# S5's parameters on GpSimd, and partition changes by TensorE products

## The chip, the core and the metric

The kernel runs on one core of one Trainium2 chip. The metric is the device time of one execution in microseconds (us). The core has a matrix engine (TensorE, PE in the profile; PEld is its weight load), three engines for elementwise work (VectorE or DVE, ScalarE or ACT, GpSimd or POOL) and a queue engine for transfers (SyncE or SP). Each of them takes its instructions in the order in which they stand in its queue, and waits at semaphores for the others. SBUF is the on-chip memory of 128 partitions, PSUM holds what TensorE produces.

## The reference

A decoder of two layers over 272 tokens (16 learned ones and 256 of the input), width 1024, in float32. In every layer the normed input is projected by one large matrix `w_in`; four mixers work on slices of the result, each is gated and projected back, and a squared-ReLU MLP follows.

```python
def s5_mixer(u, lam_re, lam_im, b_re, b_im, c_re, c_im, d_skip, log_step, glu_w, glu_b):
    step = exp(log_step)[:, None]
    mag = exp(lr * step)
    ab_re, ab_im = mag * cos(li * step), mag * sin(li * step)
    inv = 1.0 / (lr * lr + li * li)
    co_re = ((ab_re - 1.0) * lr + ab_im * li) * inv
    co_im = (ab_im * lr - (ab_re - 1.0) * li) * inv
    # bb = co * b (complex); x_t = ab * x_{t-1} + bb u_t; y_t = Re(c x_t)
    y = y.reshape(bsz, t, BRANCH_WIDTH) + d_skip * u
    y = gelu(y)
    a, gt = split(y @ glu_w + glu_b, 2, axis=-1)
    return a * sigmoid(gt)

def rotary(x):      # retention's q and k, heads of 64
    x1, x2 = x[..., :half], x[..., half:]
    return concatenate([x1 * cos - x2 * sin, x1 * sin + x2 * cos], axis=-1)
```

S5's parameters (`ab`, `co`, and powers of `ab`) depend on the weights alone: 32 groups of 64 states, for both layers. The other two mixers are a Mamba-2 SSD and HGRN2.

## The kernel before, in words

Activations are kept with features on the partitions and the 272 tokens along the free axis. Weights arrive in 336 chunks of 128 x 1024 floats (`wst`), in a fixed order (`ORDER`): in each layer HGRN's inputs, SSD's, S5's, HGRN's gate, then gates and branch products of the mixers, retention's inputs, the GLU, the output product and the MLP. Each chunk is split into a high part on ACT (`whi`, L325) and a low part on DVE (`wlo`, L327), with three and two buffers. Every product with a weight chunk is then three matmuls, high by high, high by low and low by high (L344, L345, L347). So for each chunk PE needs one ACT and one DVE operation, and these stand in their engines' queues among all the other work.

The program is written in the order hgrn_in, hgrn, ssd_in, ssd, s5_params (layer 0 only, for both layers), s5_in, s5, gates and merges, ret_in, ret, glu. The order of the instructions in each queue isn't that order: a planner (`schedule_with_timeline_sim`) sets it from its own estimate of times, with offsets of priority (`PS`, `PD` for chunks), and it mixes chunks with the mixers' small steps. Once set, each queue's order is fixed.

`s5_params` (L833) computes the parameters on [128, 2, 16] slices: sine and cosine by polynomials, powers of `ab` in `pw`, coefficients `c5`, and tables `eb`, `ea` that are doubled in length step by step. Its helpers `tt` and `ts` are a two-input operation (L845) and one with scalars (L849, L851). HGRN's level updates (L1324) and SSD's decay products (L1442) are on POOL.

`s5` (L1090) runs four batches of four pairs of groups. `s5_prep` loads raw weights (`s5a`, DMA issued on ACT's queue), makes `bs`, `cx` and the tables `s5e` (`s5_table`, on POOL); `s5_run` multiplies by the input (L1109, into two PSUM banks of tag "mb"), runs the recurrence as two scans on DVE and adds up the output Y (L1148). Within Y a partition holds (position in a block of 4 tokens, feature), so after every second batch `s5_out` (L1150) applies Gelu on ACT and copies 16 pieces of 32 partitions to other partitions of `yf`, eight on ACT (L1162) and eight on DVE (L1160). At the end `split` (L362 on ACT, L364 on DVE) makes the high and low parts that the GLU reads much later.

`ret_in` (L1476) copies q and k out of PSUM, loads two tables of cosines and sines, and on POOL makes four products of 32 partitions each that write to the neighbouring 32 partitions (L1496), one product over all (L1497) and two adds (L1500 for q, L1501 for k into `kpad`).

Of the kernel before, what the change touches and what calls it, by code (L numbers as in the profile page):

```python
# [12 lines left out]
AF = mybir.ActivationFunctionType  # L13
ALU = mybir.AluOpType
# [54 lines left out]

CONSTS = {}  # L70
_n = 0
for _name, _w in (("ident", 128), ("ones", 128), ("cen", 128), ("m432", 432), ("he", 1), ("ho", 1), ("le", 1), ("lo", 1),
                  ("rh", 1), ("rl", 1), ("r1", 1)):
    CONSTS[_name] = (_n, _w)
    _n += _w
# [18 lines left out]
def shape_constants():  # L94
    f = np.float32
    p = np.arange(128)
    c = np.zeros((128, NCONST), f)

    def put(name, a):
        o, w = CONSTS[name]  # L100
        c[:, o:o + w] = a

    put("ident", np.eye(128))
    put("ones", 1.0)
    put("cen", np.eye(128) - 1.0 / 128)
    t = np.arange(T)
    m = np.zeros((128, 432))
    m[:, :272] = t[None, :] >= p[:, None]
    m[:, 272:416] = t[None, 128:] >= 128 + p[:, None]
    m[:, 416:] = (t[None, 256:] >= 256 + p[:, None]) & (p[:, None] < 16)  # L110
    put("m432", m)
    h, r = p // 16, p % 16

    for nm, odd in (("e", 0), ("o", 1)):
        low = np.where((r == 6) & (h % 2 == odd), -1.0, 0.0)
        put("l" + nm, low[:, None])
        put("h" + nm, (np.where((r == 0) & (h % 2 == odd), -1.0, 0.0) - low)[:, None])
    put("rl", (r >= 6)[:, None])
    put("rh", np.where(r < 6, 1.0, -1.0)[:, None])
    put("r1", ((r == 0) | (r == 6))[:, None])  # L120
    sc = np.zeros((128, NSSDC), f)
    s = np.arange(384)
    chunk, used = r % 6 - 1, (r % 6 > 0) & (r < 12)
    blk = used[:, None] & ((s[None, :] // CH) == chunk[:, None]) & (s[None, :] < T)
    sc[:, 0:384] = blk & (h[:, None] % 2 == 0)
    sc[:, 384:768] = blk & (h[:, None] % 2 == 1)
    sc[:, 768:1040] = used[:, None] & (t[None, :] >= CH * chunk[:, None])
    sc[:, 1040:1312] = (t[None, :] % CH) != 0

    gam = 1.0 - np.exp2(-5.0 - np.arange(4.0))  # L130
    inv = (10000.0 ** (-np.arange(32.0) / 32)).astype(f)
    ang = (t[:, None].astype(f) * inv[None, :]).astype(f).astype(np.float64)
    rot = np.zeros((128, 2, 4, T))
    for i in range(2):
        for q in range(4):
            head = 2 * i + q // 2
            rows = slice(32 * q, 32 * q + 32)
            up = gam[head] ** t.astype(np.float64)
            for k in range(2):
                g = (1.0 / up) * 64 ** -0.5 if k else up  # L140
                rot[rows, 0, 2 * k + i] = np.cos(ang).T * g

                sgn = 1.0 if q % 2 == 0 else -1.0
                rot[rows, 1, 2 * k + i] = sgn * np.sin(ang).T * g
    lv = np.zeros((128, len(LEVELS), 128), np.int32)
    x = p[:, None] ^ p[None, :]
    for i, hh in enumerate(LEVELS):
        if hh == 0:
            lv[:, i] = x == 0
        else:  # L150
            lv[:, i] = (x >= hh) & (x < 2 * hh) & (p[None, :] > p[:, None])
    return c, sc, rot.astype(f).reshape(128, 2 * 4 * T), lv.reshape(128, -1)
# [81 lines left out]
class Net:  # L234
# [598 lines left out]
    def s5_params(self):  # L833

        nc = self.nc
        v = nc.vector
        DD = [128, DEPTH, 16]
        S, S2 = self.s5t("s5b").rearrange("p (i l q) -> p i l q", l=DEPTH, q=16), self.s5t("s5c")
        d4 = S2[:, 256:512]
# [2 lines left out]
        lr, li, step = col("lr"), col("li"), self.stp[:, :, 0:16]  # L842

        def tt(o, a, b, op):
            v.tensor_tensor(out=o, in0=a, in1=b, op=op)  # L845

        def ts(o, a, s1, op0, s2=None, op1=None):
            if op1 is None:
                v.tensor_scalar(out=o, in0=a, scalar1=s1, scalar2=None, op0=op0)  # L849
            else:  # L850
                v.tensor_scalar(out=o, in0=a, scalar1=s1, scalar2=s2, op0=op0, op1=op1)  # L851

        it = iter([S[:, i] for i in range(34)] + [S2[:, i] for i in range(8)])
        new = lambda: next(it)
# [5 lines left out]
        k, r, z, sn, cs = new(), new(), new(), new(), new()  # L860
        ts(k, th, 0.6366197723675814, ALU.mult, MAGIC, ALU.add)
        ts(k, k, MAGIC, ALU.subtract)
        v.scalar_tensor_tensor(out=r, in0=k, scalar=-PIO2[0], in1=th, op0=ALU.mult, op1=ALU.add)
        v.scalar_tensor_tensor(out=r, in0=k, scalar=-PIO2[1], in1=r, op0=ALU.mult, op1=ALU.add)
        v.scalar_tensor_tensor(out=r, in0=k, scalar=-PIO2[2], in1=r, op0=ALU.mult, op1=ALU.add)
        tt(z, r, r, ALU.mult)
        ts(sn, z, SIN_C[0], ALU.mult, SIN_C[1], ALU.add)
        tt(sn, sn, z, ALU.mult)
# [6 lines left out]
        ts(cs, cs, COS_C[2], ALU.add)  # L875
        tt(cs, cs, z, ALU.mult)
        tt(cs, cs, z, ALU.mult)
        v.scalar_tensor_tensor(out=cs, in0=z, scalar=-0.5, in1=cs, op0=ALU.mult, op1=ALU.add)
        ts(cs, cs, 1.0, ALU.add)

        q, odd, ss, sc, d = new(), new(), new(), new(), new()
        ts(q, k, 0.25, ALU.mult, MAGIC, ALU.add)
        ts(q, q, MAGIC, ALU.subtract)
        v.scalar_tensor_tensor(out=q, in0=q, scalar=-4.0, in1=k, op0=ALU.mult, op1=ALU.add)
        tt(d, q, q, ALU.mult)
        ts(odd, d, 1.0, ALU.is_equal)
        ts(d, d, 4.0, ALU.is_equal)
# [17 lines left out]
        tt(cs, Bv, sc, ALU.mult)  # L905

        pw = self.cp.tile([128, 2, 5, DEPTH, 16], F32, name="s5p")
        v.memset(pw[:, 0, 0], 1.0)
        v.memset(pw[:, 1, 0], 0.0)
        tt(pw[:, 0, 1], mag, cs, ALU.mult)  # L910
        tt(pw[:, 1, 1], mag, sn, ALU.mult)

# [7 lines left out]

        P = lambda i: (pw[:, 0, i], pw[:, 1, i])
        cmul(*P(2), *P(1), *P(1))
        cmul(*P(3), *P(2), *P(1))
        cmul(*P(4), *P(2), *P(2))

        c5 = self.cp.tile([128, 2, 4, DEPTH, 16], F32, name="s5c")
        inv, t = new(), new()
# [12 lines left out]
        tt(t, am, li, ALU.mult)  # L940
        tt(cI, cI, t, ALU.subtract)
        tt(cI, cI, inv, ALU.mult)
        for s in (2, 1, 0):
            cmul(c5[:, 0, s], c5[:, 1, s], cR, cI, *P(3 - s))

        self.eb = self.cp.tile([128, 2, DEPTH, 16, 8], F32, name="s5eb")
        self.ea = self.cp.tile([128, 2, DEPTH, 16, 9], F32, name="s5ea")
# [2 lines left out]
        cmul(*e1, *e2, *e2)  # L950
        cur = e1
        for t, n in ((self.eb, 8), (self.ea, 9)):
            v.memset(t[:, 0, :, :, 0:1], 1.0)
            v.memset(t[:, 1, :, :, 0:1], 0.0)
            w = 1
            while w < n:
                k = min(w, n - w)
                sh = [128, DEPTH, 16, k]
                f = [c.unsqueeze(3).to_broadcast(sh) for c in cur]
                src, dst = ([t[:, r, :, :, o:o + k] for r in range(2)] for o in (0, w))  # L960
                tm = d4[:, 0:32 * k].rearrange("p (l q k) -> p l q k", l=DEPTH, q=16)
                tt(dst[0], src[0], f[0], ALU.mult)
                tt(tm, src[1], f[1], ALU.mult)
                tt(dst[0], dst[0], tm, ALU.subtract)
                tt(dst[1], src[0], f[1], ALU.mult)
                tt(tm, src[1], f[0], ALU.mult)
                tt(dst[1], dst[1], tm, ALU.add)
                if t is self.eb or 2 * w < n:
                    nxt = e8 if cur is not e8 else e2
                    cmul(*nxt, *cur, *cur)  # L970
                    cur = nxt
                w *= 2
# [105 lines left out]
        return W.rearrange("p a q c -> p (a q) c")  # L1078

    def s5(self, l, W):  # L1080
        yf = self.slot(6, [128, 4, 68, 4])
        for b in range(4):
            Y = self.cmy[:, 2:4].rearrange("p a (q c) -> p (a q) c", q=4)
            if l and b == 0:
                prep = self.ahead
            else:
                fs, prep = self.s5_prep(l, b, self.decay if l and b == 1 else self.begin)
                for f in fs:
                    f()
            self.s5_run(l, b, W, prep, Y[:, 4 * (b % 2):4 * (b % 2) + 4])  # L1090
            if b % 2:
                self.s5_out(b - 1, Y, yf)
        yf = yf.rearrange("p a c s -> p a (c s)")
        gh, gl = self.slot(9, [128, 4, T], F32R), self.slot(7, [128, 4, T], F32R)
        for i in range(4):
            self.split(yf[:, i], gh[:, i], gl[:, i])
        return gh, gl

    def s5_run(self, l, b, W, prep, Y):
# [47 lines left out]
                                 rhs=st[:, r, q, 0:68], start=False, stop=(r == 1))  # L1147
        v.tensor_tensor(out=Y, in0=yp, in1=du, op=ALU.add)  # L1148

    def s5_out(self, b, Y, yf):  # L1150

        nc = self.nc
        Y = Y.rearrange("p q c -> p (q c)")
        nc.scalar.activation(Y, Y, AF.Gelu_apprx_tanh)
        G = Y.rearrange("p (a q c) -> p a q c", a=2, q=4)
        for q in range(4):
            for s in range(4):
                o, i = yf[32 * q:32 * q + 32, b:b + 2, :, s], G[32 * s:32 * s + 32, :, q, :]
                if q % 2:
                    nc.vector.tensor_copy(o, i)  # L1160
                else:
                    nc.scalar.activation(o, i, AF.Copy)  # L1162

    def glu(self, l, x, ks, sl):
        nc = self.nc
# [313 lines left out]
    def ret_in(self, l, u, t0):  # L1479
# [11 lines left out]
        for i in range(2):  # L1491
            self.load_after(rot[i], self.io["rot"].rearrange("p (c k t) -> p c k t", c=2, k=4)[:, i], qk[:, 0:1, 0:1])
        sw = self.slot(13, [128, 4, T])
        for q in range(4):
            a, b = slice(32 * q, 32 * q + 32), slice(32 * (q ^ 1), 32 * (q ^ 1) + 32)
            g.tensor_tensor(out=sw[b], in0=qk[a], in1=rot[1][a], op=ALU.mult)  # L1496
        g.tensor_tensor(out=qk, in0=qk, in1=rot[0], op=ALU.mult)  # L1497
        qf, k = self.slot(14, [128, 4, T]), self.kpad[1]
        q = qf[:, 0:2]
        g.tensor_tensor(out=q, in0=qk[:, 0:2], in1=sw[:, 0:2], op=ALU.add)  # L1500
        g.tensor_tensor(out=k[:, :, 0:T], in0=qk[:, 2:4], in1=sw[:, 2:4], op=ALU.add)  # L1501
        v01, v2 = self.slot(0, [128, 2, 4, 128]), self.vpad[0].rearrange("p (i e) -> p i e", i=4)
        for i in range(4):
            ps = self.proj(l, O_RV + 128 * i, u)
# [47 lines left out]
```

## Time and profile before

| | |
|---|---|
| median of 3 runs | 1277.0 us (1274.56 to 1277.59) |
| profiled execution | 1277.68 us |
| its span | 1275.9 us |
| PE busy | 1216.1 us, 95% |
| DVE busy | 893.0 us, 70% |
| ACT busy | 694.2 us, 54% |
| POOL busy | 411.0 us, 32% |

The profile is of one execution. Busy time counts an engine's own instructions, without its waits. Matmuls overlap in the pipeline, so the mean of one (about 0.29 us) is longer than the distance to the next (about 0.125 us). A matmul in float32 appears as two records in the trace, each with its weight load; the three products with weight chunks are single records. The chain of waits follows the execution back from its last instruction, at each step to what released it.

### The profile page before, as it was taken

What the parts mean: (1) busy time and instruction counts of PE and PEld (TensorE: products, weight loads), DVE (VectorE), ACT (ScalarE), POOL (GpSimd) and SP (SyncE); (2) the same over time, 40 slices, a digit from 0 to 9 for tenths busy, and PEclk for the clock granted to TensorE, in tenths of its full rate; (3) what the DMA queues carried; (4) which work ended last, traced back from release to release, by engine and by line L of the source; (5) the groups of instructions that cost most, each with busy time, mean ns of one, the idle gap of its engine ahead of it and who ended that gap; (6) DMA issues with size and microseconds to landing.
All of it is one profiled execution on the core that took longest, in us unless ns stands there. A gap on an engine that the chain in (4) does not pass through costs nothing.

```text
span 1275.9 us, 24312 instructions
## 1 busy us (share of the span) xinstructions
PE 1216.1 (95%) x9534; PEld 1174.6 (92%) x9534; DVE 893.0 (70%) x1480; ACT 694.2 (54%) x1219; POOL 411.0 (32%) x422
## 2 busy tenths in 40 slices
PE   8999998879999989999989999988999998999997
PEld 7999897879999989999979998987999998999996
DVE  8999989885637675544468995898656487655444
ACT  7446746443745665544455558354647546665442
POOL 2452467668002142200024333575170031322001
PEclk9999999989999989999989999998999998999998
DMA  6423232344354535555434332333444553555552
GB/s 238 160 98 104 101 123 99 108 136 145 135 175 173 176 110 178 173 175 178 170 108 143 126 123 97 123 111 114 146 150 149 184 179 136 169 188 189 182 184 98
DMA packets 53187, 186.69 MB, mean 146 GB/s; under 512 B 6096, under 2 KB 7248, under 8 KB 53072
## 3 DMA queue, kind: packets, MB, share of 16 engines
q1 hardware_dynamic: 50480, 179.40, 41.2%
q10 hardware_dynamic: 2592, 5.74, 1.4%
q8 instruction: 75, 1.23, 0.4%
q14 instruction: 40, 0.33, 0.1%
HBM read 184.06 MB, written 1.05 MB: 145 GB/s over the span
## 4 chain that ended last, share of the span: by engine, by line
PE 76%; DVE 13%; issue 4%; POOL 3%; ACT 2%; DMA 1%; SPq 0%; DVEq 0%; ACTq 0%; POOLq 0%
PE g L347 22%; PE g L344 22%; PE g L345 22%; DVE wlo L327 3%; PE mb L726 1%; PE ma L1263 1%; PE mb L717 1%; POOL S L1496 1%; DVE h L604 1%; DMA s5a<-in_bc 1%; DVE big_npom L601 1%; DVE s5a L1012 1%; ACT whi L325 1%; PE ma L726 1%; PE mb L1109 1%
## 5 line engine op out<-in xcount | busy, mean ns | idle before, releaser
L327 DVE TENSOR_TENSOR wlo<-wst,whi 128x1024 fp32r<-128x1024 f32 x336 | 438.5, 1306 | 259.1 <-PE g L347 220.8
L325 ACT ACTIVATE whi<-wst 128x1024 fp32r<-128x1024 f32 x336 | 355.8, 1060 | 365.3 <-PE g L345 287.6
L347 PE MATMUL g<-xh_u,wlo 128*128 128x272 f32 (+1 forms) x1024 | 299.7, 294 | 16.0 <-DVE wlo L327 15.8
L344 PE MATMUL g<-xh_u,whi 128*128 128x272 f32 (+1 forms) x1024 | 299.5, 293 | 0.6 <-ACT early L1068 0.4
L345 PE MATMUL g<-xl_u,whi 128*128 128x272 f32 (+1 forms) x1024 | 297.8, 291 | 0.0
L344 PE MATMUL g<-S,whi 128*128 128x272 f32 (+1 forms) x832 | 236.0, 288 | 4.6 <-ACT S L541 4.1
L347 PE MATMUL g<-S,wlo 128*128 128x272 f32 (+1 forms) x808 | 230.0, 288 | 1.7 <-DVE wlo L327 1.7
L345 PE MATMUL g<-S,whi 128*128 128x272 f32 (+1 forms) x768 | 220.4, 289 | 2.2 <-DVE S L552 1.9
L347 PEld LDWEIGHTS g<-xh_u,wlo 128*128 128x128 f32 x1024 | 195.7, 192 | 21.0 <-DVE wlo L327 18.2
L344 PEld LDWEIGHTS g<-xh_u,whi 128*128 128x128 f32 x1024 | 196.5, 192 | 2.6 <-ACT early L1068 0.7
L345 PEld LDWEIGHTS g<-xl_u,whi 128*128 128x128 f32 x1024 | 196.5, 192 | 1.5 <-issue 1.2
L344 PEld LDWEIGHTS g<-S,whi 128*128 128x128 f32 x832 | 157.1, 190 | 5.3 <-ACT S L541 4.5
L347 PEld LDWEIGHTS g<-S,wlo 128*128 128x128 f32 x808 | 151.9, 189 | 2.6 <-DVE wlo L327 2.2
L345 PEld LDWEIGHTS g<-S,whi 128*128 128x128 f32 x768 | 145.8, 190 | 4.1 <-DVE S L552 4.0
L345 PE MATMUL g<-xl_npm,whi 128*128 128x272 f32 (+1 forms) x512 | 147.7, 291 | 1.2 <-DVE xl_npm L552 1.2
L344 PE MATMUL g<-xh_npm,whi 128*128 128x272 f32 (+1 forms) x512 | 143.6, 289 | 2.4 <-ACT xh_npm L541 2.4
L347 PE MATMUL g<-xh_npm,wlo 128*128 128x272 f32 (+1 forms) x496 | 140.5, 288 | 0.0
L345 PEld LDWEIGHTS g<-xl_npm,whi 128*128 128x128 f32 x512 | 99.1, 193 | 1.9 <-DVE xl_npm L552 1.7
L344 PEld LDWEIGHTS g<-xh_npm,whi 128*128 128x128 f32 x512 | 96.7, 193 | 2.9 <-ACT xh_npm L541 2.9
L677 POOL TENSOR_TENSOR acc<-acc,tmp 128x272 f32<-128x272 f32 (+1 forms) x48 | 38.9, 828 | 186.0 <-DVE tmp L676 186.0
L347 PEld LDWEIGHTS g<-xh_npm,wlo 128*128 128x128 f32 x496 | 94.2, 192 | 0.2
L507 POOL TENSOR_TENSOR tmp<-tmp 128x272 f32<-128x272 f32 (+1 forms) x64 | 45.7, 714 | 137.3 <-DVE wlo L327 79.5
(377 smaller groups left out, 2184.4 us busy)
## 6 DMA issues: line engine op xcount, KB each, us to landing
wst<-in_w SPq DMA_DIRECT2D x336, 512.0 KB, 3.5
S<-in_rot ACTq DMA_DIRECT2D x4, 544.0 KB, 6.8
s5a<-in_bc ACTq DMA_DIRECT2D x8, 256.0 KB, 3.4
h<-in_h SPq DMA_DIRECT2D x4, 272.0 KB, 5.5
S<-in_ssdc ACTq DMA_DIRECT2D x2, 384.0 KB, 4.4
dtc<-in_ssdc ACTq DMA_DIRECT2D x2, 272.0 KB, 4.7
out<-h SPq DMA_DIRECT2D x2, 256.0 KB, 2.8
S<-in_lvl SPq DMA_DIRECT2D x1, 448.0 KB, 7.2
```

Source lines behind the costliest of these rows:

```text
L325: a = nc.scalar.activation(hi, st, AF.Copy)
L327: nc.vector.tensor_tensor(out=lo, in0=st, in1=hi.bitcast(F32), op=ALU.subtract)
L344: self.nc.tensor.matmul(out, lhsT=a, rhs=r, start=st, stop=False)
L345: self.nc.tensor.matmul(out, lhsT=a, rhs=s, start=False, stop=False)
L347: end = self.nc.tensor.matmul(out, lhsT=b, rhs=r, start=False, stop=en)
L507: nc.gpsimd.tensor_tensor(out=q, in0=a, in1=a, op=ALU.mult)
L601: e.tensor_tensor(out=mw[:, k], in0=mw[:, k], in1=r, op=ALU.mult)
L604: e.tensor_tensor(out=self.h[:, k, sl], in0=self.h[:, k, sl], in1=mw[:, k], op=ALU.add)
L677: nc.gpsimd.tensor_tensor(out=a, in0=a, in1=t, op=ALU.add)
L717: nc.tensor.matmul(ps[:, c0:c0 + T - q0], lhsT=k[b, 128 * s:128 * s + 128], rhs=q[b, q0:T], start=True, stop=True)
L726: nc.tensor.matmul(out[:, t:T], lhsT=v01[s] if s < 2 else v2, rhs=P[:, p0:p0 + T - t], start=s == 0, stop=s == 2)
L1012: e.tensor_tensor(out=tmp, in0=X[1 - r], in1=F[1], op=ALU.mult)
```

## The change

S5's parameters: the helpers now issue on GpSimd; `scalar_tensor_tensor` becomes two operations each, the third and fourth powers are made in one complex product, and the three `c5` products in one. The reciprocal and the exponential for `mag` stay on VectorE. S5's outputs: `s5_out` no longer copies; for each half of Y it makes 16 matmuls with 32 columns of the identity as weights, which bring the four pieces of 32 partitions to their place in a PSUM bank. After the second batch two ACT copies bring the banks to `yf`; after the fourth the banks are split directly. Retention's rotary: a constant matrix "swap" exchanges the halves by one matmul per tile, DVE multiplies by the sine table (whose sign is now that of the receiving half), POOL multiplies by the cosine table and adds, tile by tile.

```diff
@@ constants
+    put("swap", np.eye(128)[p ^ 32])
...
-                sgn = 1.0 if q % 2 == 0 else -1.0
+                sgn = -1.0 if q % 2 == 0 else 1.0
@@ s5_params
         def tt(o, a, b, op):
-            v.tensor_tensor(out=o, in0=a, in1=b, op=op)
+            g.tensor_tensor(out=o, in0=a, in1=b, op=op)
 
         def ts(o, a, s1, op0, s2=None, op1=None):
...
-                v.tensor_scalar(out=o, in0=a, scalar1=s1, scalar2=s2, op0=op0, op1=op1)
+                g.tensor_scalar(out=o, in0=a, scalar1=s1, scalar2=s2, op0=op0, op1=op1)
...
-        v.scalar_tensor_tensor(out=r, in0=k, scalar=-PIO2[0], in1=th, op0=ALU.mult, op1=ALU.add)
-        v.scalar_tensor_tensor(out=r, in0=k, scalar=-PIO2[1], in1=r, op0=ALU.mult, op1=ALU.add)
-        v.scalar_tensor_tensor(out=r, in0=k, scalar=-PIO2[2], in1=r, op0=ALU.mult, op1=ALU.add)
+        for i, c in enumerate(PIO2):
+            ts(z, k, -c, ALU.mult)
+            tt(r, z, r if i else th, ALU.add)
...
-        cmul(*P(3), *P(2), *P(1))
-        cmul(*P(4), *P(2), *P(2))
+        sh = [128, 2, DEPTH, 16]
+        d = d4[:, 0:64].rearrange("p (i l q) -> p i l q", i=2, l=DEPTH)
+        cmul(pw[:, 0, 3:5], pw[:, 1, 3:5], pw[:, 0, 1:3], pw[:, 1, 1:3],
+             *[x.unsqueeze(1).to_broadcast(sh) for x in P(2)])
...
-        for s in (2, 1, 0):
-            cmul(c5[:, 0, s], c5[:, 1, s], cR, cI, *P(3 - s))
+        sh = [128, 3, DEPTH, 16]
+        d = d4[:, 0:96].rearrange("p (i l q) -> p i l q", i=3, l=DEPTH)
+        cmul(c5[:, 0, 0:3], c5[:, 1, 0:3], *[pw[:, r, 3:0:-1] for r in range(2)],
+             *[x.unsqueeze(1).to_broadcast(sh) for x in (cR, cI)])
@@ s5
-            if b % 2:
-                self.s5_out(b - 1, Y, yf)
-        yf = yf.rearrange("p a c s -> p a (c s)")
+            if b == 1:
+                for i, ps in enumerate(self.s5_out(Y)):
+                    nc.scalar.activation(yf[:, i], ps, AF.Copy)
         gh, gl = self.slot(9, [128, 4, T], F32R), self.slot(7, [128, 4, T], F32R)
-        for i in range(4):
-            self.split(yf[:, i], gh[:, i], gl[:, i])
+        cs = lambda a: a.rearrange("p (c s) -> p c s", s=4)
+        for i in range(2):
+            self.split(yf[:, i], cs(gh[:, i]), cs(gl[:, i]))
+        for i, ps in enumerate(self.s5_out(Y)):
+            self.split(ps, cs(gh[:, 2 + i]), cs(gl[:, 2 + i]))
@@ s5_out
-        for q in range(4):
+        out = []
+        for a in range(2):
+            ps = self.bank("mb")[:, :T].rearrange("p (s c) -> p s c", s=4)
             for s in range(4):
-                o, i = yf[32 * q:32 * q + 32, b:b + 2, :, s], G[32 * s:32 * s + 32, :, q, :]
-                if q % 2:
-                    nc.vector.tensor_copy(o, i)
-                else:
-                    nc.scalar.activation(o, i, AF.Copy)
+                for q in range(4):
+                    nc.tensor.matmul(ps[32 * q:32 * q + 32, s], lhsT=self.c("ident")[:, 32 * s:32 * s + 32],
+                                     rhs=G[:, a, q], start=True, stop=True)
+            out.append(ps.rearrange("p s c -> p c s"))
+        return out
@@ ret_in
-        for q in range(4):
-            a, b = slice(32 * q, 32 * q + 32), slice(32 * (q ^ 1), 32 * (q ^ 1) + 32)
-            g.tensor_tensor(out=sw[b], in0=qk[a], in1=rot[1][a], op=ALU.mult)
-        g.tensor_tensor(out=qk, in0=qk, in1=rot[0], op=ALU.mult)
...
-        g.tensor_tensor(out=q, in0=qk[:, 0:2], in1=sw[:, 0:2], op=ALU.add)
-        g.tensor_tensor(out=k[:, :, 0:T], in0=qk[:, 2:4], in1=sw[:, 2:4], op=ALU.add)
+        for i in range(4):
+
+            ps = self.bank()[:, :T]
+            nc.tensor.matmul(ps, lhsT=self.c("swap"), rhs=qk[:, i], start=True, stop=True)
+            nc.vector.tensor_tensor(out=sw[:, i], in0=ps, in1=rot[1][:, i], op=ALU.mult)
+            g.tensor_tensor(out=qk[:, i], in0=qk[:, i], in1=rot[0][:, i], op=ALU.mult)
+            g.tensor_tensor(out=q[:, i] if i < 2 else k[:, i - 2, 0:T], in0=qk[:, i], in1=sw[:, i], op=ALU.add)
```

## Rows read from the trace of the kernel before

**Rows 1.** The page: busy time, share of the span, instructions; the chain by engine.

```profile
PE 1216.1 (95%) x9534; PEld 1174.6 (92%) x9534; DVE 893.0 (70%) x1480; ACT 694.2 (54%) x1219; POOL 411.0 (32%) x422
PE 76%; DVE 13%; issue 4%; POOL 3%; ACT 2%; DMA 1%; SPq 0%; DVEq 0%; ACTq 0%; POOLq 0%
```

**Rows 2.** View by stretches: length, busy us (instructions) by engine, clock, DMA.

```profile
core 0: us, PE busy (x) PEld busy (x) DVE busy (x) ACT busy (x) POOL busy (x), PEclk, DMA share, GB/s
44.00:160.00 116.00, 113.66 (x897) 106.85 (x896) 115.69 (x353) 70.92 (x140) 42.88 (x34) 1.00 0.32 110
200.00:280.00 80.00, 65.64 (x495) 62.42 (x496) 76.16 (x108) 42.71 (x82) 56.21 (x57) 0.97 0.33 111
280.00:320.00 40.00, 40.00 (x285) 37.74 (x284) 21.27 (x23) 13.95 (x24) 27.61 (x15) 0.93 0.44 149
820.00:900.00 80.00, 69.59 (x517) 65.52 (x518) 70.60 (x102) 38.58 (x74) 55.28 (x61) 0.91 0.34 112
900.00:940.00 40.00, 38.53 (x310) 37.00 (x309) 22.17 (x28) 23.86 (x45) 17.16 (x6) 1.00 0.47 159
```

**Rows 3.** PE's timeline: start, us, instruction, idle time before it and releaser.

```profile
229.46 0.39 PE L347 MATMUL g<-xh_u,wlo 128*128 128x272 f32 x1 [2.86 <-DVE wlo L327]
279.21 0.59 PE L347 MATMUL g<-xh_u,wlo 128*128 128x272 f32 x1 [2.69 <-DVE wlo L327]
864.53 0.39 PE L344 MATMUL g<-yh_hg,whi 128*128 128x256 f32 x1 [2.61 <-DVE acc L673]
909.12 0.38 PE L347 MATMUL g<-xh_u,wlo 128*128 128x256 f32 x1 [1.47 <-DVE wlo L327]
```

**Rows 4.** DVE's timeline, the copies of s5_out ahead of three waits.

```profile
222.69 2.38 DVE L1160 COPY S<-S 32x136 f32<-32x136 f32 x8
275.24 2.66 DVE L1160 COPY S<-S 32x136 f32<-32x136 f32 x8
905.45 2.36 DVE L1160 COPY S<-S 32x136 f32<-32x136 f32 x8 [0.96 <-ACT S L1154]
```

**Rows 5.** The chain of waits, 854 to 870 us: start, us, what.

```profile
855.85 0.34 ACT S L1162
...
857.19 4.57 DMA s5a<-in_bc
```

**Rows 6.** View by stretches behind three of the waits, with the granted clock.

```profile
229.00:235.00 6.00, 5.54 (x32) 5.55 (x33) 6.00 (x12) 1.38 (x3) 2.30 (x3) 0.72 0.32 107
278.00:286.00 8.00, 6.79 (x32) 6.79 (x33) 4.22 (x5) 3.32 (x6) 0.92 (x1) 0.57 0.65 226
864.00:870.00 6.00, 5.47 (x33) 5.34 (x34) 6.00 (x10) 4.27 (x7) 2.79 (x2) 0.72 0.30 97
```

**Rows 7.** View by stretches of line 845 alone (DVE, two-input parameter operations).

```profile
0.00:160.00 160.00, 29.81 (x162) 1.00 0.41 140
```

**Rows 8.** View by stretches of line 327 alone, 28 chunks in each layer.

```profile
51.30:190.90 139.60, 37.38 (x28) 1.00 0.34 113
699.10:839.50 140.40, 36.30 (x28) 1.00 0.33 112
```

**Rows 9.** POOL's timeline, HGRN's four smallest products of totals.

```profile
38.30 2.42 POOL L1237 TENSOR_TENSOR S<-S 128x68 f32<-128x68 f32 x4
```

**Rows 10.** Two DVE lines: count, duration in ns min/median/max, first and last start.

```profile
L1012 DVE TENSOR_TENSOR s5a<-s5a,s5c x16: 660/692/1462, 111.7 to 868.0; 128x512 f32<-128x512 f32 x16
L673 DVE SCALAR_TENSOR_TENSOR acc<-S,g x16: 406/423/426, 204.4 to 870.3; 128x272 f32<-128x272 f32 x8, 128x256 f32<-128x256 f32 x8
```

**Rows 11.** The chain of waits, three runs of float32 products.

```profile
125.47 1.76 PE ma L726 x12
138.69 0.92 PE mb L726 x8
246.00 0.89 PE mb L1109 x8
```

**Rows 12.** POOL's timeline of the rotary products, and the wait for its last result.

```profile
285.08 13.78 POOL L1496 TENSOR_TENSOR S<-S,S 32x1088 f32<-32x1088 f32 x4 [8.50 <-ACT S L1489]
PEld ma L717 <- POOL kpad L1501: 0.3, 1, 0.3
```

More of the change, by code (lines that the diff above doesn't have):

```diff
@@ L71 @@
 _n = 0
-for _name, _w in (("ident", 128), ("ones", 128), ("cen", 128), ("m432", 432), ("he", 1), ("ho", 1), ("le", 1), ("lo", 1),
+for _name, _w in (("ident", 128), ("ones", 128), ("cen", 128), ("swap", 128), ("m432", 432), ("he", 1), ("ho", 1), ("le", 1), ("lo", 1),
                   ("rh", 1), ("rl", 1), ("r1", 1)):
@@ L835, in s5_params @@
         nc = self.nc
-        v = nc.vector
+        v, g = nc.vector, nc.gpsimd
         DD = [128, DEPTH, 16]
@@ L844, in tt @@
         def tt(o, a, b, op):
-            v.tensor_tensor(out=o, in0=a, in1=b, op=op)
+            g.tensor_tensor(out=o, in0=a, in1=b, op=op)
         def ts(o, a, s1, op0, s2=None, op1=None):
             if op1 is None:
-                v.tensor_scalar(out=o, in0=a, scalar1=s1, scalar2=None, op0=op0)
+                g.tensor_scalar(out=o, in0=a, scalar1=s1, scalar2=None, op0=op0)
             else:
-                v.tensor_scalar(out=o, in0=a, scalar1=s1, scalar2=s2, op0=op0, op1=op1)
+                g.tensor_scalar(out=o, in0=a, scalar1=s1, scalar2=s2, op0=op0, op1=op1)
         it = iter([S[:, i] for i in range(34)] + [S2[:, i] for i in range(8)])
@@ L877, in s5_params @@
         tt(cs, cs, z, ALU.mult)
-        v.scalar_tensor_tensor(out=cs, in0=z, scalar=-0.5, in1=cs, op0=ALU.mult, op1=ALU.add)
+        ts(z, z, -0.5, ALU.mult)
+        tt(cs, cs, z, ALU.add)
         ts(cs, cs, 1.0, ALU.add)
@@ L883, in s5_params @@
         ts(q, q, MAGIC, ALU.subtract)
-        v.scalar_tensor_tensor(out=q, in0=q, scalar=-4.0, in1=k, op0=ALU.mult, op1=ALU.add)
+        ts(q, q, -4.0, ALU.mult)
+        tt(q, q, k, ALU.add)
         tt(d, q, q, ALU.mult)
@@ L907, in s5_params @@
         pw = self.cp.tile([128, 2, 5, DEPTH, 16], F32, name="s5p")
-        v.memset(pw[:, 0, 0], 1.0)
-        v.memset(pw[:, 1, 0], 0.0)
+        g.memset(pw[:, 0, 0], 1.0)
+        g.memset(pw[:, 1, 0], 0.0)
         tt(pw[:, 0, 1], mag, cs, ALU.mult)
@@ L942, in s5_params @@
         tt(cI, cI, inv, ALU.mult)
-        for s in (2, 1, 0):
-            cmul(c5[:, 0, s], c5[:, 1, s], cR, cI, *P(3 - s))
+        sh = [128, 3, DEPTH, 16]
+        d = d4[:, 0:96].rearrange("p (i l q) -> p i l q", i=3, l=DEPTH)
+        cmul(c5[:, 0, 0:3], c5[:, 1, 0:3], *[pw[:, r, 3:0:-1] for r in range(2)],
+             *[x.unsqueeze(1).to_broadcast(sh) for x in (cR, cI)])
+        d = new()
         self.eb = self.cp.tile([128, 2, DEPTH, 16, 8], F32, name="s5eb")
@@ L952, in s5_params @@
         for t, n in ((self.eb, 8), (self.ea, 9)):
-            v.memset(t[:, 0, :, :, 0:1], 1.0)
-            v.memset(t[:, 1, :, :, 0:1], 0.0)
+            g.memset(t[:, 0, :, :, 0:1], 1.0)
+            g.memset(t[:, 1, :, :, 0:1], 0.0)
             w = 1
@@ L1080, in s5 @@
     def s5(self, l, W):
-        yf = self.slot(6, [128, 4, 68, 4])
+        nc = self.nc
+        yf = self.slot(6, [128, 2, 68, 4])
         for b in range(4):
@@ L1148, in s5_run, with s5_out @@
         v.tensor_tensor(out=Y, in0=yp, in1=du, op=ALU.add)
-    def s5_out(self, b, Y, yf):
+    def s5_out(self, Y):
         nc = self.nc
```

## The prediction

> **What bounds the kernel now.** I read the page first: TensorE (PE) is busy for 95% of the span and 76% of the chain that ended last is PE, but 13% of it is VectorE (DVE) [rows 1]. PE is the bound over the whole, so the question is where it still waits and for whom. The view by stretches answers that: it waits little up to 160 us (2.3 us in 44 to 160), and then in the two S5 stages, 200 to 280 us in layer 0 (80.0 - 65.6 = 14.4 us) and 820 to 900 in layer 1 (10.4 us), where DVE is busy for 76.2 and 70.6 of 80 us. Right behind them, in 280 to 320, PE is full [rows 2]. Third the timelines of PE and DVE at the ends of the S5 stages. PE stands still for 2.86, 2.69, 2.61 and 1.47 us behind the four calls of s5_out [rows 3]. Ahead of three of these waits DVE has run the eight small copies of L1160 back to back, 2.38, 2.66 and 2.36 us [rows 4], and the next split (wlo, L327), for which PE waits, is queued behind them. Ahead of the other one, at 864.5 us, ScalarE's (ACT's) own copies of L1162 hold back a DMA issue on ACT's queue: from 855.85 to 857.19 the chain is those copies, then 4.57 us of DMA, then DVE [rows 5]. Fourth the clock: after three of the waits PE is granted the lower of its levels (1.2 of 2.4 GHz) for a while. Mean clocks of 0.72 over 6 us, 0.57 over 8 and 0.72 over 6 make (1 - clock) x length = 1.7, 3.4 and 1.7 us of full-speed work lost [rows 6].
>
> **The parameters.** Of 190 small DVE operations, 149 two-input ones, 22 with a scalar and 6 memsets remain, on GpSimd (POOL); only the reciprocal and mag's exponential stay on DVE. DVE's 162 two-input operations take 29.8 us of its time, all before 160 us [rows 7]; with the rest about 34 us go. What is that worth? The same 28 weight chunks (from the first SSD projection on) are split within 139.6 us in layer 0, with parameters in between, and within 140.4 in layer 1, which has none [rows 8]. So DVE's load there isn't on the path: I take 0 for its removal, and at most the 2.3 us for which PE idles in that stretch. Cover: PE's own chunks.
>
> The other side is POOL. Four dependent two-input operations of 68 elements and fewer per partition took 2.42 us, 0.60 each [rows 9]; on DVE the price is 29.8 / 162 = 0.18. Between these ends I take 0.40, near the middle, since the parameters have 32 elements mostly, and 64 to 128 at the end: 171 x 0.40 = 68 us (31 and 103 at the ends). POOL has 116.0 - 42.9 = 73.1 us free from 44 us, where hgrn's first products leave its queue, to 160 [rows 2], about where S5's first tables are due. It just fits. Queued behind them on POOL are hgrn's 16 level updates (L1324) and SSD's decay products; each can find one operation of 0.40 us ahead of it, 0 to 16 x 0.40 = 6.4 us. DVE, which takes part in the same steps, is then less loaded, and PE has other chunks queued between; I take 0.5.
>
> A DVE operation with two SBUF inputs depends on what runs beside it: L1012 takes 0.66 us at best and 1.46 at worst, while L673, one of whose inputs is in PSUM, stays within 0.406 and 0.426 [rows 10]. The Trainium skill says this in GPSIMD Engine Reference, Specifications: the two engines share SBUF interfaces, and DVE's instructions with two SBUF inputs are among those that contend. The trace agrees. By that rule POOL's 68 us more slow down the splits, on which PE depends; by the trace DVE has 34 us of new slack there. I charge nothing and give it to a rival.
>
> **S5's outputs.** Four calls (two a layer), each without its 16 copies. Gains: 2.4 and 2.7 us in layer 0, 1.3 us (857.19 - 855.85) at the first call of layer 1, and 1.5 us at its last, where the wait is shorter than the copies [rows 3 to 5]: 7.9 us, less if something else makes the next split late (none at the low end). In layer 0 the wait is then nearly gone, and with it, I take it, the low clock behind it: 1.7 + 3.4 = 5.1 us [rows 6]. In layer 1 half of the wait stays, and I leave its clock as it is. Bounds: 0 and 6.8.
>
> Added: 32 matmuls a call, 64 records of 68 columns (fp32 makes two records of one matmul). No row shows 32-wide weights into four column groups. Upper bound: records of 68 columns with 128-wide weights, 0.89 / 8 = 0.111 us, so 7.1 us a call. By columns: two full-width heads of 864 record columns each take 1.76 us, so 1.02 ns a column; two 64-wide heads, which write to the two halves of the array, take 0.92 us in all, 1.91 times as fast [rows 11]. 64 x 68 x 1.02 = 4.4 us in single file, 4.4 / 1.91 = 2.3 if the groups overlap as these halves do, 1.1 if all four do. I take 2.3, as nearest to the row with column groups: 9.2 us for four calls. The last call of layer 1 falls where PE is nearly full (38.5 of 40 us [rows 2]) and is paid, 2.3. The other three fall where PE still waits for DVE (14.4 - 5.1 = 9.3 us left in layer 0, 10.4 - 1.3 = 9.1 in layer 1). In the middle of a wait they cost nothing, otherwise their time; I charge a third of 6.9, 2.3, and if that cover is gone 4.6 more. Sum 4.6. New waits: these matmuls wait for the Gelu on ACT, and V's products of the next batch, which use the same two banks, may wait for their evictions. Weight chunks are queued behind them on PE. I take 0, since one call has at most the 2.9 us of today's waits to lose.
>
> The Trainium skill's TensorEngine Tiling, Theoretical Speedup, gives up to four times for 32-wide tiles. By that a call is 1.1 us, four are 4.4, and the sum would come out 2.4 us lower. The trace shows 1.91 for two halves, and nothing for four.
>
> **The rotary halves.** POOL's four partition-moving products go (13.78 us in layer 0), and the wide product and adds become eight narrow ones. What waits for them is little: PE 0.3 us for kpad in layer 1 [rows 12]. Four products with "swap" are 4 x 2 x 272 record columns x 1.02 ns = 2.2 us a layer. They stand where PE is full in both layers [rows 2], so they are paid: 4.4 - 0.3 = 4.1. At the low end they fall into gaps and cost nothing, at the high end each starts late by a bank, 6. DVE's four products from PSUM, some 0.42 us each by L673, lie beside its idle half (21.3 of 40 us busy).
>
> **Sum.** -7.9 - 5.1 + 4.6 + 4.1 + 0.5 = -3.8 us. The profiled execution took 1277.68 us (span 1275.9 and 1.8 around it), so 1273.9; it stands 0.7 above the median of 1277.0, so 1273.2.
>
> **Rivals.** *A, larger gain:* the four groups overlap fully (1.1 us a call, all in gaps but the last: 1.1 instead of 4.6), and the added activity keeps the clock up behind layer 1's wait as well (-1.7), with the 2.3 us of the stretch before 160 gained: 1273.2 - 3.5 - 1.7 - 2.3, about 1266. For it: DVE's burst is the last thing ahead of each wait. Against: DVE is busy for 95% of layer 0's stage without the copies' help.
>
> *B, a plain exchange:* each call puts 2.3 us of PE work exactly where PE waited, nothing hides it and the clock stays low: -7.9 + 9.2 + 4.1 + 0.5 = +5.9 with the clock as before, +0.8 with layer 0's clock back; about 1278. For it: removed waits and added work are of one size.
>
> *C, slower, POOL takes the place of DVE:* it decides from 73.1 / 171 = 0.43 us for one operation. At 0.60 the parameters need 103 us, 30 more than are free, S5's tables start late and each of the 16 level updates finds 0.60 us ahead of it, 9.6 us, while the splits, slowed by contention, take the rest of DVE's slack. With 9.6 instead of 0.5 the sum is 1282; with some of S5's late start showing, 1285. For it: [rows 9], and the skill's rule above. Against: the fit at 0.40, and that PE has long fill.
>
> *D, slower, products in single file:* at 7.1 us a call three calls outgrow their gaps: 4 x (7.1 - 2.3) = 19 more, a third of it hidden: 1286. Against: the 64-wide pair in [rows 11].
>
> **Chances.** The forecast 0.40 (own range 1268 to 1278), A 0.17, B 0.15, C 0.18, D 0.10. What a measurement of this kernel tells from no change is 0.3%, 3.8 us, and the forecast sits on that bound. Faster: 0.22 of the forecast, all of A, 0.05 of B, so 0.44; same: 0.16 + 0.08 of B + 0.04 of C + 0.01 of D = 0.29; slower 0.27. The range reaches from below A to C and D: 1261 to 1286.
>
> **What would show it.** Right: no burst of 32-partition copies; PE's four waits under 1 us; clock at 1.0 around layer 0's end of S5; the 64 records of a call in about 2.3 us; POOL over 90% busy from 44 to 160 with operations near 0.40 us, and S5's first tables still by about 160. Wrong: PE waits in 44 to 160 above 2.3 us with POOL as releaser (C), a call over 4 us (D), or the waits under other names, for Gelu or a bank (B).

## The result, and the profile after

The changed kernel takes 1305.2 us (median of 4 runs, 1304.1 to 1307.1) against 1276.7 for the kernel before, beside it on the same chip: ratio 1.0222, interval 1.0201 to 1.0243. The forecast was 1273.2 with a range up to 1286, so it is 28.6 us slower where 3.8 us less were forecast, and further out than any rival.

The page's busy times, to be read beside [rows 1]: PE has 14.3 us more, DVE 30.7 less, POOL 20.7 more, and the span is 26.1 longer. PE is still the only engine that is nearly full, with 95% as before; the totals don't tell where the time went.

```profile
PE 1230.4 (95%) x9806; PEld 1187.1 (91%) x9806; DVE 862.3 (66%) x1266; ACT 683.3 (52%) x1192; POOL 431.7 (33%) x601
```

The view by stretches does, with the columns of [rows 2]: 44 to 160 first, then the S5 stage of layer 1, which comes 31 us later than before, and the 40 us behind it.

```profile
44.00:160.00 116.00, 90.72 (x651) 83.85 (x651) 78.71 (x142) 44.99 (x96) 91.36 (x201) 0.90 0.23 73
851.00:931.00 80.00, 73.62 (x630) 69.73 (x630) 69.03 (x97) 38.53 (x73) 54.38 (x62) 0.96 0.37 126
931.00:971.00 40.00, 40.00 (x366) 37.77 (x366) 18.83 (x25) 19.10 (x34) 9.61 (x11) 1.00 0.42 145
```

In 44 to 160, where PE idled for 2.3 us before, it now idles for 116.0 - 90.7 = 25.3, and its mean clock is 0.90 instead of 1.00, another 0.10 x 116 = 11.6 us of full-speed work. DVE has 37 us less to do there (78.7 against 115.7) and POOL 48 more. In layer 1, which makes no parameters, PE does more in the same 80 us (73.6 against 69.6) and the clock is 0.96 against 0.91. So the loss is in layer 0's first 160 us. The weight splits (wlo) show the same: the 33rd starts 46.2 us later than before (197.0 against 150.8), the first of layer 1 is 31.5 us late (676.8 against 645.3) and the last 26.3 (1284.9 against 1258.6), so the S5 stages even give some of it back. PE's waits in 36 to 160 (line waited at, releaser, us in total, times, longest) name HGRN's products at L1277 and L1269, waiting for its level updates on POOL (L1338) or for DVE's part of the same steps, 18.8 us in these four lines:

```profile
PE ma L1277 <- POOL S L1338: 6.9, 3, 3.7
PE ma L1269 <- POOL S L1338: 5.2, 1, 5.2
PE ma L1277 <- DVE S L1284: 4.1, 1, 4.1
PE ma L1269 <- DVE S L1340: 2.6, 1, 2.6
```

The 16 level updates themselves, one line for each kernel (count, ns min/median/max, first and last start, forms), before and after:

```profile
L1324 POOL TENSOR_TENSOR S<-S,S x16: 632/1018/4142, 61.1 to 113.5; 128x272 f32<-128x272 f32 x8, 128x256 f32<-128x256 f32 x8
```

```profile
L1338 POOL TENSOR_TENSOR S<-S,S x16: 615/858/1445, 72.2 to 137.2; 128x272 f32<-128x272 f32 x8, 128x256 f32<-128x256 f32 x8
```

The updates are no slower (median 858 against 1018 ns), but the first starts 11.1 us later and the last 23.7. Is it their queue or a late input? An update changes what a product of PE (L1263 before, L1277 after) has just read, so it may start when that product ends. First before, then after, PE's products with POOL's first update behind them:

```profile
59.03 1.95 PE L1263 MATMUL ma<-S,S 128*128 128x128 f32 x16
61.06 1.05 POOL L1324 TENSOR_TENSOR S<-S,S 128x272 f32<-128x272 f32 x1 [4.93 <-PE ma L1263]
```

```profile
62.08 1.95 PE L1277 MATMUL ma<-S,S 128*128 128x128 f32 x16
72.23 0.89 POOL L1338 TENSOR_TENSOR S<-S,S 128x272 f32<-128x272 f32 x1
```

Before, POOL stood idle and took up the update 0.08 us behind the product's end (60.98). Now the product ends at 64.03, only 3.1 us later, and POOL, which isn't idle ahead of the update, comes to it 8.2 us behind that. One level further on PE itself stands still for it:

```profile
89.93 1.05 PE L1277 MATMUL ma<-S,S 128*128 128x128 f32 x8
99.82 0.89 POOL L1338 TENSOR_TENSOR S<-S,S 128x272 f32<-128x272 f32 x1
100.77 1.47 PE L1277 MATMUL ma<-S,S 128*128 128x128 f32 x8 [3.67 <-POOL S L1338]
```

So it goes with all twelve updates behind products of this line: 4.3 to 10.0 us behind their products, 6.8 on average, with no idle time of POOL ahead of any; before it was 0.1 to 0.4 in ten cases, and 1.9 and 2.8 in two. The queue holds them. What stands ahead of them is seen in the stretches of L846 alone, POOL's two-input parameter operations, up to the first update and from there to the last:

```profile
36.00:72.20 36.20, 17.52 (x64) 0.93 0.37 122
72.20:137.30 65.10, 35.07 (x81) 0.85 0.20 61
```

One operation stands in both counts. All 149 take 56.0 us, 0.38 each. With the 22 operations with a scalar (10.9 us) the parameters take 66.9 us of POOL; the prediction had 68.

One place shows how the queue carries the delay to other engines. POOL's timeline, first before, then after (start, us, instruction, idle time before it): L274, in the changed kernel L275, is a one-column copy. It orders a DMA of SSD's tables that ScalarE (ACT) issues.

```profile
55.83 0.19 POOL L274 COPY S<-dts 128x1 f32<-128x1 f32 x1 [11.70 <-ACT dts L1350]
```

```profile
59.40 2.08 POOL L846 TENSOR_TENSOR s5b<-s5b 128x32 f32<-128x32 f32 x7
...
61.85 1.26 POOL L846 TENSOR_TENSOR s5p<-s5b 128x32 f32<-128x32 f32 x1
...
66.68 0.19 POOL L275 COPY S<-dts 128x1 f32<-128x1 f32 x1
```

ACT's and DVE's timelines of the changed kernel go on from there:

```profile
59.54 0.41 ACT L1366 ACTIVATE dts<-dts 128x272 f32<-128x272 f32 x1
66.90 0.33 ACTq L277 DMA_DIRECT2D S<-in_ssdc  x1
67.75 1.28 ACT L1369 ACT_TABLE_LOAD   x1 [7.80 <-POOL s5b L846]
...
61.78 1.23 DVE L328 TENSOR_TENSOR wlo<-wst,whi 128x1024 fp32r<-128x1024 f32 x1 [0.41 <-PE g L348]
69.51 0.48 DVE L1370 TENSOR_TENSOR dts<-dts 128x272 f32<-128x272 f32 x1 [6.51 <-ACT dts L1369]
```

Before, POOL stood idle and waited for the data. Now it reaches the copy 10.9 us later, ACT stands at the DMA issue for 7.80 us, DVE behind ACT for 6.51, and HGRN's steps are queued behind both: PE's 4.1 us for L1284, above, end when DVE comes out of this wait.

### The profile page after: what moved, and what is told of

The parts are those of the page before. It is cut to its first block, busy times and chain, and to the rows that moved or that the text cites. A ratio compares the mean times of both kernels' runs of the same rounds, so it can differ in the third digit from the quotient of the medians.

```text
span 1302.0 us, 24800 instructions
## 1 busy us (share of the span) xinstructions
PE 1230.4 (95%) x9806; PEld 1187.1 (91%) x9806; DVE 862.3 (66%) x1266; ACT 683.3 (52%) x1192; POOL 431.7 (33%) x601
## 5 line engine op out<-in xcount | busy, mean ns | idle before, releaser
L328 DVE TENSOR_TENSOR wlo<-wst,whi 128x1024 fp32r<-128x1024 f32 x336 | 431.6, 1285 | 278.1 <-PE g L348 227.8
```

Of the source, the lines that this page charges most:

```text
L328: nc.vector.tensor_tensor(out=lo, in0=st, in1=hi.bitcast(F32), op=ALU.subtract)
```

## The experiments

**Which part of the change.** Three runs add one part each to the kernel before. The outputs alone:

```
+ nc.tensor.matmul(ps[32*q:32*q+32, s], lhsT=ident[:, 32*s:32*s+32], rhs=G[:, a, q], ...)
- nc.vector.tensor_copy(o, i)  /  nc.scalar.activation(o, i, AF.Copy)
```

> The kernel before with only S5's outputs by TensorE products. The 64 records of a call took about 1.0 us in the trace of the changed kernel, so four calls cost at most 4.4 us and relieve the four waits of 9.6 us and part of the low clock: 1266 to 1271. If the products only take the place of the waits: 1277 +- 2.

Measured 1272.6 against 1277.1 (ratio 0.9958, 0.9942 to 0.9975), 1.6 us above the expected range and faster than both kernels. The profiled execution took 1269.7, near the lowest of its nine (1269.5 to 1274.9), so its trace shows more gain than the median. The gain lies in layer 1: its first weight split starts 0.5 us earlier than before, its first split for the down projection 8.0 earlier. In layer 0 the copies are gone too, but PE's 9.5 us of waits for wlo in 200 to 285 became 5.1, and 3.0 at a new place. Its layer 1 stage (820 to 900) in stretches, 72.5 of 80 us and the full clock against 69.6 and 0.91:

```profile
820.00:900.00 80.00, 72.47 (x647) 68.76 (x646) 69.34 (x98) 39.12 (x74) 53.35 (x60) 1.00 0.37 124
```

The rotary halves alone (partition-moving products on POOL out, four "swap" products and DVE products in):

> The kernel before with only the rotary halves by TensorE products. By the price of the prediction 8 products of 0.5 us on a full TensorE: 1279 to 1281. If the shorter GpSimd chain (13.8 us of partition-moving products gone) lets something else start earlier: 1272 to 1276.

Measured 1278.8 (ratio 1.0012, 0.9998 to 1.0026): +1.7 us, no difference that can be told.

The parameters alone on POOL, in the changed kernel's form:

> The kernel before with only the parameters' operations moved to GpSimd in the new form. If they are the cause: the whole loss and what the other two parts gave back, 28.6 + 5 to 10, so 1309 to 1316 us, with HGRN's level updates behind runs of parameter operations in GpSimd's queue. If the TensorE products are the cause: 1274 to 1280.

Measured 1316.6 (ratio 1.0303, 1.0281 to 1.0324): +39.5 us. This part makes the loss, and more: the three parts add up to 39.5 - 4.5 + 1.7 = 36.7, where the change costs 28.6. With both TensorE edits in, the parameters on POOL cost 32.8 (1305.2 against 1272.4, a run below). No run shows where the difference comes from.

**How the parameters on POOL cost it.** The changed kernel with every parameter operation behind the last level update:

```
+ with self.tc.issue_after(self.last_up.ins):
      self.s5_params()
```

> The changed kernel with every parameter operation held back until the last of HGRN's level updates of layer 0; their number, engine and total time are as in the change. Queue theory: HGRN is as quick as before, the parameters run from about 115 us on, S5 starts some 20 us later beside other chunks: 1266 to 1280. If the total GpSimd time or the late S5 is what costs: 1290 or more.

Measured 1285.3 (1.0073, 1.0059 to 1.0088). The expected end was missed by 5 us, but the stretch is healed. PE's and the others' 44 to 160, and the level updates' line:

```profile
44.00:160.00 116.00, 111.33 (x858) 103.60 (x856) 87.53 (x174) 68.51 (x134) 67.98 (x135) 0.99 0.34 110
```

```profile
L1340 POOL TENSOR_TENSOR S<-S,S x16: 614/920/3488, 60.5 to 112.6; 128x272 f32<-128x272 f32 x8, 128x256 f32<-128x256 f32 x8
```

PE's idle time there is 4.7 us instead of 25.3, and the updates run from 60.5 to 112.6, as before the change. The operations are the same, on the same engine, and the 149 take 55.7 us instead of 56.0: 20 of the 28.6 us come from where they stand, not from their number or price. The rest shows later: S5's tables are ready only near 190 us, and PE waits 5.4 us at one place for S5's preparation.

Next I took single victims out of POOL's queue. Level updates of layer 0 on VectorE:

> The changed kernel with HGRN's level updates of layer 0 on VectorE; the parameters stay on GpSimd. Queue theory (the updates wait behind runs of parameter operations): the loss goes, 1266 to 1276 us, and HGRN's first output chunk comes at about 110 us as before instead of 153. Contention theory (busy GpSimd slows VectorE's two-input operations, the splits above all): VectorE now has more to do beside a GpSimd as busy, 1295 or more.

Measured 1303.1 (1.0208). A miss: ACT's and DVE's waits of 7.8 and 6.5 us at the SSD tables stay, and ACT waits for 12.5 us at one place of S5's preparation. The two ordering copies on ScalarE, level updates left on POOL:

```
- nc.gpsimd.tensor_copy(out[cell], dep[cell])
+ nc.scalar.activation(out[cell], dep[cell], AF.Copy)
```

> The kernel after, with the two one-column copies that order the SSD tables' DMAs in layer 0 (GpSimd; ScalarE issues the DMA behind them) made on ScalarE. Theory: those copies stand behind some 70 parameter operations, hold ScalarE's queue for 7.8 us at the DMA issue, and with it VectorE's (6.5 us at the softplus), so this stretch of the loss goes: 1294 to 1301. Rival: the level updates stand behind the same parameter operations, which decide alone, so the first of them stays at 72 us: 1302 to 1306.

Measured 1304.8 (1.0216): nothing, the rival. The two waits at the SSD tables are gone, but DVE now waits for 8.9 us one step further on, for SSD's next small operation on POOL, which stands behind the same queue, and the first update still starts at 73.3 us. Both together:

> The kernel after with both: level updates of layer 0 on VectorE and the two ordering copies on ScalarE, so that nothing of HGRN's levels or of the SSD's decay tables waits in GpSimd's queue behind the parameters except the products that make the running totals. Theory (several in-order waits, each enough by itself): 1284 to 1296, since with only the levels moved it was 1303.1. Rival (shared port or another cause): 1300 or more.

Measured 1299.4 (1.0172, 1.0149 to 1.0195): 6 of the 28.6 us, between theory and rival. The first update starts at 62.9, the last still at 140.1, and PE idles 22.7 us in 44 to 160. DVE's two longest waits are now for S5's preparation, which needs late parameters and, in DVE's queue, stands ahead of HGRN's steps:

```profile
44.00:160.00 116.00, 93.29 (x698) 88.49 (x693) 85.16 (x170) 52.14 (x108) 74.54 (x181) 0.87 0.27 86
```

```profile
DVE s5g L1022 <- POOL s5c L849: 9.5, 1, 9.5
DVE s5b L1022 <- POOL s5c L849: 7.0, 1, 7.0
```

I also tried to hold that preparation back behind the last parameter operation, with the updates on either engine:

> The kernel after with layer 0's level updates on VectorE and, besides, S5's preparation in layer 0 issued only after the last parameter operation. In-order theory (a late parameter's users stand at the head of VectorE's and ScalarE's queues and hold what is behind them): the level updates end near 115 us and the time falls from 1303 to 1282 to 1295, the rest being S5's late start. Rival (GpSimd's operations slow VectorE through a shared port): stays at 1300 or more.

> The kernel after, with S5's preparation in layer 0 issued only after the last parameter operation; level updates stay on GpSimd behind runs of parameter operations. If GpSimd's own queue carries most of the loss: level updates still end after 130 us, 1298 to 1304. If the users' waits on VectorE and ScalarE carry most: 1283 to 1295.

Measured 1300.8 and 1304.3. Neither says anything on the users: the hold names an operation of another engine, and DVE's wait at L1019 was still there in both (5.9 and 5.6 us). All victims moved at once was not tried.

**The form.** The changed form on VectorE, where the parameters were: first as it stands in the changed kernel, then with the fused operations of the kernel before kept and only the products merged.

> The changed kernel with the parameters' operations back on VectorE, in the new smaller number; outputs and rotary stay TensorE products. If the loss comes from the parameters on GpSimd, by whatever mechanism, the time is below the kernel before: layer 1, which has no parameters, took 5.1 us less from its first chunk to the first chunk of its down product, and layer 0 should gain about as much, so 1265 to 1272 us. If the loss comes from the TensorE products, the time stays at 1290 or more.

> As the first of these kernels (parameters on VectorE, TensorE products kept), with the five fused scalar-tensor-tensor operations kept as well and the merged complex products: the fewest VectorE operations. All theories: within 2 us of that kernel, 1264 to 1271; if it is clearly below it, VectorE's load in layer 0 was on the path after all.

Measured 1285.3 (1.0057, 1.0037 to 1.0076) and 1280.2 (1.0029, 1.0018 to 1.0039). Both missed: fewer operations on the old engine are slower than the kernel before. Two runs divide it: the old parameters with both TensorE edits, and the merged ones without these edits.

> The kernel after, with the parameters exactly as before (VectorE, separate products); both TensorE edits stay. Theory M: the merged form of the parameters is what cost 15 us of layer 0 where they were on VectorE with both TensorE edits; then the two edits add as they did alone, -4.1 and +1.6, and this runs at 1271 to 1277. Rival: the two TensorE edits together disturb the queues of layer 0, whoever makes the parameters; then 1279 to 1285. First S5 chunks in layer 0 tell where: the stretch from the SSD input's chunks to the gate of HGRN is 58 us before, 73 with the merged form.

> The kernel before, with only the parameters' products merged (twelve operations fewer on VectorE, in a different order); outputs and rotary as before. Theory M: the merged form alone costs 8 to 14 us, so 1285 to 1291. Rival (interplay with the TensorE edits): 1275 to 1278, since the parameters were hidden before and remain so.

Measured 1272.4 (0.9967, 0.9953 to 0.9981) and 1287.5 (1.0081, 1.0060 to 1.0102). The merged form alone costs 10.6 us. Stretch of the two-input parameter operations on DVE, 60 to 112 us, in the kernel before and in this one:

```profile
60.00:112.00 52.00, 4.99 (x19) 1.00 0.31 104
```

```profile
60.00:112.00 52.00, 9.74 (x44) 0.93 0.26 84
```

With the chain shorter, 44 instead of 19 of them come among HGRN's steps. That looked like the cause, so I held the tables (the second half of the parameters) behind the last level step; the first attempt named POOL's update, which left DVE's queue nearly as it was, the second an operation of DVE itself.

> Both TensorE edits, merged parameters on VectorE as in the 1280.2 us kernel, but the second half of the parameters (the two decay tables) issued only after layer 0's last level update, as the kernel before happened to have it. Theory: the merged form loses because 55 instead of 22 of its operations fall between HGRN's level updates on a saturated VectorE; held back, it runs at 1268 to 1275. Rival: the merged form itself is what costs (larger operations, later S5); then 1279 to 1286.

> As the run before, but the decay tables are held behind layer 0's last level operation on VectorE itself, so that in VectorE's own queue no parameter operation at all stands between the level steps from the third on (the hold on GpSimd's update moved none: 114 and 135 parameter operations stood ahead of the ninth and the last update, as in the 1280.2 us kernel). Theory: the merged form costs its time by the operations that it puts between the level steps; 1268 to 1275. Rival: the form itself or S5's later start costs as much; 1278 to 1286.

Measured 1280.7 and 1281.5. In the second nearly all of them are out of the stretch, four left, and nothing is gained:

```profile
60.00:112.00 52.00, 1.30 (x4) 0.93 0.27 90
```

So the number of these operations between the steps is not the cause, and this theory falls. The last three runs ask whether it is one of the merges or the order in general.

```
- cmul(*P(3), *P(2), *P(1)); cmul(*P(4), *P(2), *P(2))      # e16: same products, other order
+ cmul(*P(4), *P(2), *P(2)); cmul(*P(3), *P(2), *P(1))
- for s in (2, 1, 0):
+ for s in (0, 1, 2):
```

> Both TensorE edits with the parameters exactly as before on VectorE (1272.4 us), but with two pairs of independent products written in the other order: the same operations, sizes and count. If the form and count of the operations decide, 1271 to 1274. If the parameters' cost depends on where each operation happens to stand between the level steps, it may move by several us, to 1276 or more.

> Both TensorE edits, parameters on VectorE, only the powers' two products merged (six operations fewer). If merging costs in proportion to the operations taken away, about half of the 8 us: 1275 to 1278. If one of the two merges carries it all: 1271 to 1274 or 1279 to 1283.

> Both TensorE edits, parameters on VectorE, only the three coefficient products merged (twelve operations fewer). The counterpart of the run before: about half of the loss 1275 to 1278 if proportional; 1279 to 1283 if this merge carries it all, since S5's first outer products need its result whole; 1271 to 1274 if the powers' merge does.

Measured 1276.1 (0.9997, 0.9985 to 1.0010), 1282.4 (1.0043) and 1282.3 (1.0040). The same operations in another order cost 3.7 us of the 4.5 that the two edits gain (the intervals against the kernel before do not overlap), and either merge alone costs no less than both. The loss does not go with the count. For the reordering, only the places of the operations are left as a cause. For the merges that is a reading and not shown, since they also make single operations larger and give their results all at once. Which placement does it stays open.

## Why the prediction was wrong

**The step that failed** is the second half of the parameters' part: "each can find one operation of 0.40 us ahead of it, 0 to 16 x 0.40 = 6.4 us", of which I took 0.5. An engine works its queue in order. Ahead of the first update stand 64 two-input operations since 36 us, and 80 more come before the last, which is 23.7 us late instead of 0.5 to 6.4. Each of the twelve updates that can be paired with a product was held for 4.3 to 10.0 us, not for one operation of 0.40. With the parameters behind the updates 20 us came back at an unchanged price and count. The step counted POOL's free time as if the parameters would use only that; but they are ready early and were sorted in ahead of work that comes ready late, and that work is on PE's path.

**What was not listed.** The prediction named the level updates and the decay products as queued behind the parameters. It missed the two ordering copies, and so ACT's and DVE's queues behind them, and it never asked who uses the parameters first: S5's preparation stands in DVE's and ACT's queues and holds them when its input is late. As I read it these are several holds, and each that is left keeps most of the loss: one removed brought 0 to 2 us, two brought 6. That S5's preparation is the next of them is seen in the trace of that run alone; no run took it away.

**The price and the fit** were right: 0.38 us for a two-input operation (0.40 taken), 66.9 us in all (68), below rival C's 0.43. The price was in part luck: 0.40 was the middle of 0.18 to 0.60, and the prediction had no disturbance by DVE in it. Without that one would take 0.28 (41.9 / 149, an estimate worked out below). POOL was busy for 91.4 of the 116 us, 79% and not over 90%. Rival C was nearest in its mechanism, and its sign came, PE waits with POOL as releaser. But it put its turning point on the wrong quantity and, like the forecast, one operation ahead of each update (9.6 us): with the total well inside POOL's free time the kernel is 28.6 us slower, where C gave 5 to 8.

**The worth on DVE, 0,** was right as a bound on the gain: PE idled for 2.3 us in that stretch before, and in no run did it idle for less with DVE relieved (4.7 us at best with the parameters on POOL, though DVE has 28 us less to do there). But "not on the path" is too strong for the old placement. Reordered or merged on DVE the same work costs 4 to 11 us.

**Contention,** charged at nothing, is there, on both engines. DVE's step with two SBUF inputs and one with an input in PSUM, in 60 to 140 us, before and then after:

```profile
L1326 DVE TENSOR_TENSOR S<-S,S x14: 400/419/431, 63.2 to 109.3; 128x272 f32<-128x272 f32 x8, 128x256 f32<-128x256 f32 x6
L1272 DVE COPY_PREDICATED S<-lvl,ma x24: 421/432/448, 62.5 to 100.3; 128x256 f32<-128x256 uint8 x24
```

```profile
L1340 DVE TENSOR_TENSOR S<-S,S x14: 407/462/1398, 72.7 to 131.9; 128x272 f32<-128x272 f32 x8, 128x256 f32<-128x256 f32 x6
L1286 DVE COPY_PREDICATED S<-lvl,ma x24: 426/432/449, 72.0 to 125.4; 128x256 f32<-128x256 uint8 x24
```

The first goes from 419 to 462 ns, up to 1398, the second stays. The Trainium skill's rule (GPSIMD Engine Reference, Specifications: shared SBUF interfaces, contention with DVE's two-input instructions) has the trace's agreement, as a matter of a tenth in the median of this line. The splits, which the prediction feared for, go from 1.22 to 1.25 us (medians in 44 to 160). On POOL it is more: at the prices that its two-input operations have beside an idle DVE (0.25 us at 32 elements, 0.32 at 64, 0.44 at 128; at 96 the lowest seen, 0.38) the 149 would take 41.9 us one by one, and they take 60.8 (56.0 where overlaps count once), so by this estimate DVE adds some 19 us to POOL's queue. That makes each hold longer, but it isn't what decides: behind the updates the operations took as long (55.7 us), and 20 us of the loss were gone.

**The two TensorE edits** came out as their sum said: -7.9 - 5.1 + 4.6 + 4.1 = -4.3 us forecast, -4.5 measured with the old parameters. The terms were less good. A call's 64 records take 1.15 us, not 2.3: rival A's price; so four calls paid in full come to the 4.6 us that I had charged after hiding a part. PE's rows of the changed kernel, a call of s5_out and one swap product (two records):

```profile
237.95 1.15 PE L1173 MATMUL mb<-S,cst 128*32 128x68 f32 x64 [0.33 <-ACT S L1166]
...
308.97 0.62 PE L1513 MATMUL ma<-S,cst 128*128 128x272 f32 x2
```

The outputs gained 4.5 us, where 13.0 - 4.6 = 8.4 was forecast: layer 0's 10.2 us of waits and low clock did not come back as time, layer 1's did. The rotary cost 1.7 (not clear of noise) where 4.1 was forecast. The two errors cancel, so the right sum is luck in part. The outputs alone are as fast as both edits with the old parameters (1272.6 and 1272.4); no run was faster.

## What to carry to other kernels

Free time of an engine is not room for a long chain: work that is ready early can be sorted in ahead of work that comes ready late, and if that is on the path, every operation ahead of it counts. List all that stays in the receiving engine's queue, down to one-column copies that order a DMA, and all that first uses the moved results, and see which other queues these hold. And when a kernel's order is found by a planner, run the same operations in another order before believing a few microseconds: here that alone was worth 3.7 us.

## What the runs showed of the hardware

The four 32-wide column groups overlap: 64 records of 68 columns in 1.15 us, 18 ns each. A full-width record of 68 columns takes 111 ns [rows 11], more than six times as long, so that row holds more than its columns; by columns I had put 69 ns on a record in single file, and a fourth of that is 17. Against this estimate the Trainium skill's up to four times (TensorEngine Tiling, Theoretical Speedup) is borne out.

A two-input POOL operation of 32 elements takes 0.23 to 0.27 us when DVE stands idle beside it (55 of 113). One that starts while DVE runs a split, which has two SBUF inputs, ends only behind the split. The one at 61.85 us, shown above, ended 0.11 us behind the split that ran from 61.78 for 1.23 us. Two more, POOL's and then DVE's timeline:

```profile
85.89 1.24 POOL L846 TENSOR_TENSOR s5c<-s5eb,s5b 128x32 f32<-128x32 f32 x1
109.29 1.23 POOL L846 TENSOR_TENSOR s5b<-s5b 128x32 f32<-128x32 f32 x1
```

```profile
85.74 1.27 DVE L328 TENSOR_TENSOR wlo<-wst,whi 128x1024 fp32r<-128x1024 f32 x1
108.82 1.58 DVE L328 TENSOR_TENSOR wlo<-wst,whi 128x1024 fp32r<-128x1024 f32 x1
```

In the changed kernel this holds for all seven that start within a split: 0.11 to 0.12 us behind its end with 32 elements (four), 0.17 and 0.18 with 64, 0.32 with 128. With the parameters behind the updates it holds for 12 of 13. That the split holds the operation up is read from these times; no run took the splits away.
